# Six seven-product groups for five in the two plain feed-forward stages, with the weights' sums made by accumulating DMAs

## The chip, the cores and the metric

One core of one Trainium2 chip runs the kernel. The metric is the device time in microseconds of one execution, as the median of several. TensorE is written PE in the profile, ScalarE ACT, VectorE DVE, GpSimd POOL, SyncE SP.

## The reference

Two transformer blocks of width 2048 on 256 tokens, one after the other. The first has a state-space and a delta-rule mixer and a feed-forward with a convolution. The second has two plain SwiGLU feed-forwards of hidden width 5632 with a pooling and gated-linear-attention mixer between them. The change concerns the two SwiGLU stages:

```python
def swiglu(h, w_in, w_out):
    gu = h @ w_in
    gate, up = gu[..., :D_FF], gu[..., D_FF:]
    return (jax.nn.silu(gate) * up) @ w_out

def second_block(x, ...):
    h = h + 0.5 * swiglu(rmsnorm_2(h, ffn1_norm[l]), ffn1_w_in[l], ffn1_w_out[l])
    ...
    h = h + 0.5 * swiglu(rmsnorm_2(h, ffn2_norm[l]), ffn2_w_in[l], ffn2_w_out[l])
```

## The kernel before

Every matrix product is made in float32 precision out of three products of a rounded type: an operand is split into a high part (a copy by ScalarE, L126) and a low part (a subtraction by VectorE, L127), and low by low is left out. A weight block is 128 x 1024 float32, 512 KB, loaded by SP (L85, tile wr, four buffers) and split into wh and wl (three buffers each).

A SwiGLU stage is `ffn` (L1050) with `conv_w` None. The hidden width is cut into 11 groups g of 512. `plain(g)` (L1072) makes gate and up of one group with `gemm_tg` (L190): 8 blocks each, and per block 2 k-tiles x 2 halves of the tokens x 3 products = 12 matmuls of 512 columns (L201 to L203, into ptt); it yields after every block. `down_g(c)` (L1091) multiplies one or two groups' hidden tiles (hid) by the down weights in the same manner; its blocks are 8 for chunk 0 and 16 for chunks 1 to 4.

`seven(g)` (L1124) makes the same gate and up with seven products of half size for eight: the weights of a group are a 2 x 2 of halves (gate and up columns, lower and upper half of the k-tiles), and four of the seven products take sums of those quarters against sums of quarters of x, which `x_sums` (L1105) makes once per stage in 8 steps (tiles xf, xs, sx). A group is 28 passes (L1128), each one split into sh and sl (two buffers each) and 6 matmuls of 512 columns (L1133 to L1135, into side), and 30 yields. The weights' sums are made by VectorE (`less`, L1145, into tt, two buffers) from loaded quarters (ws, L1142, three buffers): 16 subtractions a group. Each of the four k-pairs jj makes products 0, 1, 2, 3 in a row, then each makes the three products of the second half.

`together` (L1212) draws one step of the main sequence and one of the sevens in turn. Groups 3, 4, 5, 7 and 9 are sevens, the other six are plain. When a seven or a plain is done, `turn_hidden` (L1056) transposes the result on TensorE (L1062) and splits it into hid tiles; it is put into `pend`, which `gemm_tg` empties in the middle of its next product, or into `after`, which goes to `pend` when `together` ends. The order of each engine's instructions is that of the program, with splits moved ahead by a priority (L124).

Of the kernel before, what the change touches and what calls it, by code (L numbers as in the profile page):

```python
# [18 lines left out]
P = 128  # L19
T = 256  # L20
# [31 lines left out]
def tile_kernel(ctx: ExitStack, tc: tile.TileContext, A, out):  # L52
# [203 lines left out]
    def rstd_of(ps):  # L256

        r = ev.tile([P, T], F32, tag="rstd", bufs=2, name="rstd")
        a = ev.tile([P, T], F32, tag="e0", bufs=3, name="ra")
        b = ev.tile([P, T], F32, tag="e1", bufs=3, name="rb")  # L260
        ts(a, ps[:, :T], EPS, ALU.add)
        act.activation(r, ps[:, :T], AF.Sqrt, bias=epst[:, 0:1])
        newton(r, a, b)
        mul(r, r, b)
        return r
# [480 lines left out]
    def dn_conv(h0):  # L746
        for h in range(h0, h0 + 2):
            for part, t in ((0, qk[h][:, 1, :]), (1, qk[h][:, 0, :]), (2, vv[h])):
                b = 3 * h + part
                c = ev.tile([P, T], F32, tag="e1", bufs=3, name="cc")  # L750
                conv(t, None, lambda i: par("dn_conv", 4 * b + i), 4, c)
                act.activation(t, c, AF.Silu)
                yield
# [296 lines left out]
    def ffn(up, down, hs, rstd, conv_w, scale, fin, gain=None, nxt=None, before_last=None):  # L1050
        with tc.tile_pool(name="hid", bufs=2) as hd:
# [50 lines left out]

            sx = []

            def x_sums():  # L1105
                for j in range(8):
                    f = hd.tile([P, 2, T], F32, tag="g", bufs=1, name="xf")
                    s = hd.tile([P, 4, P], F32, tag="w", bufs=1, name="xs")
                    for i in range(2):
                        add(f[:, i, :], hs[j + 8 * i][:, 0, :].bitcast(F32), hs[j + 8 * i][:, 1, :].bitcast(F32))  # L1110
                    add(s[:, 0, :], f[:, 0, P:], f[:, 1, P:])
                    sub(s[:, 1, :], s[:, 0, :], f[:, 0, :P])
                    sub(s[:, 2, :], f[:, 0, :P], f[:, 0, P:])
                    sub(s[:, 3, :], f[:, 1, :P], s[:, 1, :])
# [9 lines left out]
            def seven(g):  # L1124
# [12 lines left out]
                def block(k2, half, tag=None):  # L1137
                    src = A[up][16 * g + 8 * half + k2]
                    if tag is None:
                        return load_w(src)  # L1140
                    raw = hd.tile([P, 1024], F32, tag=tag, bufs=3, name="ws")
                    sp.dma_start(out=raw, in_=src)  # L1142
                    return raw

                def less(a, b):  # L1145
                    t = hd.tile([P, 1024], F32, tag="tt", bufs=2, name="tt")
                    with tc.high_priority(offset=600):
                        sub(t, a, b)
# [8 lines left out]
                gs, w5, w6 = (hd.tile([P, 512], F32, tag=n, bufs=1, name=n) for n in ("g", "w", "w6"))  # L1157
                for jj in range(4):
                    j, fl = 2 * jj, dict(first=jj == 0, last=jj == 3)
                    b11, b12 = block(jj, 0), block(jj, 1, "ws")  # L1160
                    t1 = less(b12, b11)
                    passes(ps[0], hx(j, 0), b11, **fl)
                    if jj == 3:
                        act.copy(out=w6, in_=ps[0])
                    yield
                    b22 = block(4 + jj, 1, "ws")
                    passes(ps[1], sxs(j, 0), t1, **fl)
                    if jj == 3:
                        add(w5, ps[1], w6)
                    yield  # L1170
                    b21 = block(4 + jj, 0, "ws")
                    t2 = less(b22, t1)
                    passes(ps[2], sxs(j, 1), t2, **fl)
                    if jj == 3:
                        add(gs, ps[2], w6)
                    yield
                    t4 = less(b21, t2)
                    passes(ps[3], hx(8 + j, 1), t4, **fl)
                    if jj == 3:
                        add(w6, ps[3], w6)  # L1180
                    yield
                for jj in range(4):
                    j, fl = 2 * jj, dict(first=False, last=jj == 3)
                    passes(ps[0], hx(8 + j, 0), block(4 + jj, 0, "ws"), **fl)
                    yield
                    b22 = block(4 + jj, 1, "ws")
                    passes(ps[1], sxs(j, 3), b22, **fl)
                    yield
                    passes(ps[2], sxs(j, 2), less(b22, block(jj, 1, "ws")), **fl)
                    yield  # L1190
                rc = late[0]
                t = hd.tile([P, 2, 512], F32, tag="tt", bufs=2, name="gates")
# [3 lines left out]
                add(gs, ps[1], gs)  # L1196
                add(w5, ps[2], w5)
# [6 lines left out]
                if g == 3:  # L1204
# [5 lines left out]
            after = []  # L1210

            def together(seq, sevens):  # L1212

                side_full[0] = True
                a, b = (itertools.chain(*s) for s in (seq, sevens))
                for x, y in itertools.zip_longest(a, b):
                    pass
# [4 lines left out]
            def up_group(c):  # L1222
                tiles = []
                for i in range(max(8 * c - 4, 0), 8 * c + 4):
                    a = ev.tile([P, T], F32, tag="e1", bufs=3, name="fa")
                    b = ev2.tile([P, T], F32, tag="e2", bufs=2, name="fb")
# [22 lines left out]
            if conv_w is None:  # L1249
# [3 lines left out]
                together([first_plain, plain(1), down_g(0), plain(2), down_g(1)], [x_sums(), seven(3), seven(4)])  # L1253
                for c in range(2, 5):
                    together([plain(2 * c + 2), down_g(c)], [seven(2 * c + 1)])
# [428 lines left out]
```

## Time and profile before

| | |
|---|---|
| median of 3 runs | 3290.38 us (3289.5 to 3291.68) |
| profiled execution | 3289.64 us |
| its span | 3287.8 us |
| TensorE busy, granted clock | 99%, 0.999 of full speed |
| first SwiGLU stage | about 1540 to 2265 us of the span |
| second SwiGLU stage | about 2555 to 3287 us |
| sevens mixed in | 1577 to 2200 and 2600 to 3222 us |

A row of the profile gives an instruction's busy time, and for the idle time ahead of it what ended that. Busy times of TensorE overlap from one matmul to the next, so a distance between matmuls is read from their starts.

### The profile page before, as it was taken

The numbers are of one execution on the slowest core, as the hardware profiler recorded it, in microseconds if no ns is written. First come the engines' busy times: TensorE is split into PE (matmuls) and PEld (weight loads), VectorE is DVE, ScalarE is ACT, GpSimd is POOL, SyncE is SP. The second block draws the span as 40 slices with busy tenths as digits, with TensorE's granted clock in tenths as the row PEclk, the third lists the DMA queues.
The fourth block names the chain that finished last, engine by engine and source line by source line (L and its number), as shares of the span: only waits on it lengthen the run. The fifth ranks groups of instructions, "written<-read, shape, count | busy, mean of one in ns | idle before, by whom it ended". The sixth has DMA issues, their size and how long they took to land.

```text
span 3287.8 us, 44587 instructions
## 1 busy us (share of the span) xinstructions
PE 3265.2 (99%) x16530; PEld 2742.9 (83%) x16530; DVE 2588.5 (79%) x3758; ACT 1774.7 (54%) x2523; POOL 4.0 (0%) x22
## 2 busy tenths in 40 slices
PE   9999999999999999999999999999999999999998
PEld 8887988888888888888888888888888888888887
DVE  8999987666877767677987887875786988878876
ACT  4566666445555445455655555545555655555554
POOL 0000000000000000000000000000000000000000
PEclk9999999999999999999999999999999999999999
DMA  6445543365555555556777777765545677777774
GB/s 223 156 152 174 179 144 116 108 225 180 192 187 188 190 188 188 188 187 204 255 247 248 246 247 243 246 197 190 173 146 195 229 243 248 249 245 243 247 253 148
DMA packets 186873, 666.09 MB, mean 203 GB/s; under 512 B 20880, under 2 KB 25488, under 8 KB 186272
## 3 DMA queue, kind: packets, MB, share of 16 engines
q1 hardware_dynamic: 186080, 662.21, 61.3%
q8 instruction: 129, 2.11, 0.3%
q10 hardware_dynamic: 576, 1.05, 0.1%
q14 instruction: 88, 0.72, 0.1%
HBM read 661.08 MB, written 2.10 MB: 202 GB/s over the span
## 4 chain that ended last, share of the span: by engine, by line
PE 94%; DVE 4%; issue 1%; ACT 1%; DMA 0%; SPq 0%; DVEq 0%
PE ptt L201 18%; PE ptt L202 18%; PE ptt L203 18%; PE pt L170 13%; PE pt L172 6%; PE side L1134 4%; PE side L1135 4%; PE side L1133 4%; DVE wl L127 1%; PE pt L135 1%; PE pt L137 1%; PE pt L136 1%; PE pt L245 1%; PE side L874 1%; PE side L885 1%; PE side L620 1%
## 5 line engine op out<-in xcount | busy, mean ns | idle before, releaser
L126 ACT CAST wh<-wr 128x1024 fp32r<-128x1024 f32 x937 | 984.2, 1051 | 1221.9 <-PE ptt L203 839.4
L127 DVE TENSOR_TENSOR wl<-wr,wh 128x1024 fp32r<-128x1024 f32 x937 | 1146.1, 1223 | 539.0 <-ACT wh L126 534.2
L170 PE MATMUL pt<-h,wh 128*128 128x512 f32 x1792 | 632.1, 397 | 0.0
L172 PE MATMUL pt<-h,wl 128*128 128x256 f32 x1792 | 502.5, 281 | 0.0
L201 PE MATMUL ptt<-wh,h 128*128 128x512 f32 x1088 | 428.3, 394 | 0.0
L202 PE MATMUL ptt<-wl,h 128*128 128x512 f32 x1088 | 425.5, 391 | 0.0
L203 PE MATMUL ptt<-wh,h 128*128 128x512 f32 x1088 | 424.2, 390 | 0.0
L202 PE MATMUL ptt<-wl,hid 128*128 128x512 f32 x1040 | 409.0, 394 | 0.0
L201 PE MATMUL ptt<-wh,hid 128*128 128x512 f32 x1040 | 408.4, 393 | 0.5 <-ACT wh L126 0.5
L203 PE MATMUL ptt<-wh,hid 128*128 128x512 f32 x1040 | 408.4, 394 | 0.0
L170 PEld LDWEIGHTS pt<-h,wh 128*128 128x128 f32 x1792 | 336.3, 188 | 80.9 <-issue 1.0
L172 PEld LDWEIGHTS pt<-h,wl 128*128 128x128 f32 x1792 | 338.3, 189 | 0.6
L201 PEld LDWEIGHTS ptt<-wh,h 128*128 128x128 f32 x1088 | 204.2, 188 | 46.7 <-ACT wh L126 1.2
L203 PEld LDWEIGHTS ptt<-wh,h 128*128 128x128 f32 x1088 | 204.3, 188 | 44.0 <-issue 0.4
L202 PEld LDWEIGHTS ptt<-wl,h 128*128 128x128 f32 x1088 | 204.2, 188 | 43.4
L201 PEld LDWEIGHTS ptt<-wh,hid 128*128 128x128 f32 x1040 | 195.4, 188 | 45.7 <-ACT wh L126 1.0
L202 PEld LDWEIGHTS ptt<-wl,hid 128*128 128x128 f32 x1040 | 195.6, 188 | 44.1
L203 PEld LDWEIGHTS ptt<-wh,hid 128*128 128x128 f32 x1040 | 195.4, 188 | 43.6 <-DVE hid L368 0.5
L127 DVE TENSOR_TENSOR sl<-tt,sh 128x1024 fp32r<-128x1024 f32 x160 | 195.9, 1224 | 21.9 <-ACT sh L126 21.3
L126 ACT CAST sh<-tt 128x1024 fp32r<-128x1024 f32 x160 | 168.3, 1052 | 52.9 <-PE side L1135 48.1
L135 PE MATMUL pt<-h,wl 128*128 128x256 f32 x512 | 149.5, 292 | 0.0
L137 PE MATMUL pt<-h,wh 128*128 128x256 f32 x512 | 145.3, 284 | 0.0
(420 smaller groups left out, 4957.9 us busy)
## 6 DMA issues: line engine op xcount, KB each, us to landing
wr<-in_f_up SPq DMA_DIRECT2D x408, 512.0 KB, 4.3
wr<-in_f_down SPq DMA_DIRECT2D x265, 512.0 KB, 4.3
ws<-in_f_up SPq DMA_DIRECT2D x240, 512.0 KB, 4.3
wr<-in_w_qkv SPq DMA_DIRECT2D x48, 512.0 KB, 3.3
wr<-in_w_gs SPq DMA_DIRECT2D x32, 512.0 KB, 3.3
wr<-in_w_gd SPq DMA_DIRECT2D x32, 512.0 KB, 3.3
wr<-in_w_glu SPq DMA_DIRECT2D x32, 512.0 KB, 3.3
wr<-in_w_out SPq DMA_DIRECT2D x32, 512.0 KB, 3.3
```

The lines of the kernel that those rows point to most:

```text
L126: act.copy(out=hi, in_=raw)
L127: dve.tensor_tensor(out=lo, in0=raw, in1=hi.bitcast(F32), op=ALU.subtract)
L135: pe.matmul(ps, wl, xt[:, 0, :], start=first, stop=False)
L137: pe.matmul(ps, wh, xt[:, 0, :], start=False, stop=last)
L170: pe.matmul(ps.rearrange("p a b -> p (a b)"), hi[:, j, :], xts[k].rearrange("p a b -> p (a b)"), start=k == 0, stop=False, skip_group_chec ...
L172: pe.matmul(ps[:, 0, :], lo[:, j, :], xts[k][:, 0, :], start=False, stop=k == n - 1, skip_group_check=True)
L201: pe.matmul(pss[t], xh, hi[:, j, :], start=k == 0, stop=False)
L202: pe.matmul(pss[t], xh, lo[:, j, :], start=False, stop=False)
L203: pe.matmul(pss[t], xl, hi[:, j, :], start=False, stop=k == n - 1)
L1133: pe.matmul(ps, xh, hi[:, i, :], start=first and i == 0, stop=False, skip_group_check=True)
L1134: pe.matmul(ps, xh, lo[:, i, :], start=False, stop=False, skip_group_check=True)
L1135: pe.matmul(ps, xl, hi[:, i, :], start=False, stop=last and i == 1, skip_group_check=True)
```

## The change

Group 8 becomes a seven too, so a stage has six sevens (3, 4, 5, 7, 8, 9) and five plain groups. In a seven, `less` and the ws tiles go. A base quarter is loaded by SP into a tt tile (five buffers), and between two products GpSimd's queue adds the next quarter to the tile with an accumulating DMA, so the tile goes through base, base + one, + two, + three quarters. Since a DMA only adds, some sums have the other sign, which `x_sums` and the end of `seven` take up. The k-pairs go two by two, (0, 1) and (2, 3), with their products in turn, so that one pair's product lies between two of the other's. `together` draws the sevens from one sequence over the whole stage: 4/3 steps for each main step, 0.6 while x's sums are made. Buffers move: e1 of the pool ev goes to the stage's pool, and its other users take e0; xf, xs, gs and w5 have two buffers.

```diff
--- before.py
+++ after.py
@@ -257,7 +257,7 @@
 
         r = ev.tile([P, T], F32, tag="rstd", bufs=2, name="rstd")
         a = ev.tile([P, T], F32, tag="e0", bufs=3, name="ra")
-        b = ev.tile([P, T], F32, tag="e1", bufs=3, name="rb")
+        b = ev.tile([P, T], F32, tag="e0", bufs=3, name="rb")
         ts(a, ps[:, :T], EPS, ALU.add)
         act.activation(r, ps[:, :T], AF.Sqrt, bias=epst[:, 0:1])
         newton(r, a, b)
@@ -747,7 +747,7 @@
         for h in range(h0, h0 + 2):
             for part, t in ((0, qk[h][:, 1, :]), (1, qk[h][:, 0, :]), (2, vv[h])):
                 b = 3 * h + part
-                c = ev.tile([P, T], F32, tag="e1", bufs=3, name="cc")
+                c = ev.tile([P, T], F32, tag="e0", bufs=3, name="cc")
                 conv(t, None, lambda i: par("dn_conv", 4 * b + i), 4, c)
                 act.activation(t, c, AF.Silu)
                 yield
@@ -1100,18 +1100,19 @@
 
 
 
+
             sx = []
 
             def x_sums():
                 for j in range(8):
-                    f = hd.tile([P, 2, T], F32, tag="g", bufs=1, name="xf")
-                    s = hd.tile([P, 4, P], F32, tag="w", bufs=1, name="xs")
+                    f = hd.tile([P, 2, T], F32, tag="g", bufs=2, name="xf")
+                    s = hd.tile([P, 4, P], F32, tag="w", bufs=2, name="xs")
                     for i in range(2):
                         add(f[:, i, :], hs[j + 8 * i][:, 0, :].bitcast(F32), hs[j + 8 * i][:, 1, :].bitcast(F32))
-                    add(s[:, 0, :], f[:, 0, P:], f[:, 1, P:])
-                    sub(s[:, 1, :], s[:, 0, :], f[:, 0, :P])
+                    sub(s[:, 0, :], f[:, 1, P:], f[:, 0, P:])
+                    stt(s[:, 1, :], s[:, 0, :], -1.0, f[:, 0, :P], ALU.mult, ALU.subtract)
                     sub(s[:, 2, :], f[:, 0, :P], f[:, 0, P:])
-                    sub(s[:, 3, :], f[:, 1, :P], s[:, 1, :])
+                    stt(s[:, 3, :], f[:, 1, :P], -1.0, s[:, 1, :], ALU.mult, ALU.subtract)
                     e = []
                     for i in range(2):
                         t = hp.tile([P, 2, 2, P], F32R, tag=f"h{j + 8 * i}", name=f"sx{j}_{i}")
@@ -1134,18 +1135,12 @@
                         pe.matmul(ps, xh, lo[:, i, :], start=False, stop=False, skip_group_check=True)
                         pe.matmul(ps, xl, hi[:, i, :], start=False, stop=last and i == 1, skip_group_check=True)
 
-                def block(k2, half, tag=None):
-                    src = A[up][16 * g + 8 * half + k2]
-                    if tag is None:
-                        return load_w(src)
-                    raw = hd.tile([P, 1024], F32, tag=tag, bufs=3, name="ws")
-                    sp.dma_start(out=raw, in_=src)
-                    return raw
-
-                def less(a, b):
-                    t = hd.tile([P, 1024], F32, tag="tt", bufs=2, name="tt")
-                    with tc.high_priority(offset=600):
-                        sub(t, a, b)
+                def src(k2, half):
+                    return A[up][16 * g + 8 * half + k2]
+
+                def base(k2, half):
+                    t = hd.tile([P, 1024], F32, tag="tt", bufs=5, name="tt")
+                    sp.dma_start(out=t, in_=src(k2, half))
                     return t
 
                 def hx(k, t):
@@ -1154,67 +1149,61 @@
                 def sxs(j, c):
                     return lambda i: sx[j + i][c]
 
-                gs, w5, w6 = (hd.tile([P, 512], F32, tag=n, bufs=1, name=n) for n in ("g", "w", "w6"))
-                for jj in range(4):
-                    j, fl = 2 * jj, dict(first=jj == 0, last=jj == 3)
-                    b11, b12 = block(jj, 0), block(jj, 1, "ws")
-                    t1 = less(b12, b11)
-                    passes(ps[0], hx(j, 0), b11, **fl)
-                    if jj == 3:
-                        act.copy(out=w6, in_=ps[0])
-                    yield
-                    b22 = block(4 + jj, 1, "ws")
-                    passes(ps[1], sxs(j, 0), t1, **fl)
-                    if jj == 3:
-                        add(w5, ps[1], w6)
-                    yield
-                    b21 = block(4 + jj, 0, "ws")
-                    t2 = less(b22, t1)
-                    passes(ps[2], sxs(j, 1), t2, **fl)
-                    if jj == 3:
-                        add(gs, ps[2], w6)
-                    yield
-                    t4 = less(b21, t2)
-                    passes(ps[3], hx(8 + j, 1), t4, **fl)
-                    if jj == 3:
-                        add(w6, ps[3], w6)
-                    yield
-                for jj in range(4):
-                    j, fl = 2 * jj, dict(first=False, last=jj == 3)
-                    passes(ps[0], hx(8 + j, 0), block(4 + jj, 0, "ws"), **fl)
-                    yield
-                    b22 = block(4 + jj, 1, "ws")
-                    passes(ps[1], sxs(j, 3), b22, **fl)
-                    yield
-                    passes(ps[2], sxs(j, 2), less(b22, block(jj, 1, "ws")), **fl)
-                    yield
+                gs, w5, w6 = (hd.tile([P, 512], F32, tag=n, bufs=b, name=n) for n, b in (("g", 2), ("w", 2), ("w6", 1)))
+                for pair in ((0, 1), (2, 3)):
+                    tt = {jj: base(jj, 0) for jj in pair}
+                    for n in range(4):
+                        for jj in pair:
+                            xa = (hx(2 * jj, 0), sxs(2 * jj, 0), sxs(2 * jj, 1), hx(8 + 2 * jj, 1))[n]
+                            passes(ps[n], xa, tt[jj], first=jj == 0, last=jj == 3)
+                            if n < 3:
+                                pool_e.dma_start(out=tt[jj], in_=(src(jj, 1), src(4 + jj, 1), src(4 + jj, 0))[n],
+                                                 accum_op=ALU.add)
+                            if jj == 3 and n == 0:
+                                act.copy(out=w6, in_=ps[0])
+                            elif jj == 3:
+                                add((w5, gs, w6)[n - 1], ps[n], w6)
+                            yield
+                for pair in ((0, 1), (2, 3)):
+                    tt = {jj: base(4 + jj, 1) for jj in pair}
+                    for n in (1, 2, 0):
+                        for jj in pair:
+                            xa = (hx(8 + 2 * jj, 0), sxs(2 * jj, 3), sxs(2 * jj, 2))[n]
+                            passes(ps[n], xa, tt[jj] if n else load_w(src(4 + jj, 0)), first=False, last=jj == 3)
+                            if n == 1:
+                                pool_e.dma_start(out=tt[jj], in_=src(jj, 1), accum_op=ALU.add)
+                            yield
                 rc = late[0]
-                t = hd.tile([P, 2, 512], F32, tag="tt", bufs=2, name="gates")
+                t = hd.tile([P, 2, 512], F32, tag="tt", bufs=5, name="gates")
                 act.activation(t[:, 0], ps[0], AF.Silu, scale=rc[:, 0:1])
                 add(t[:, 1], ps[2], w6)
                 act.activation(t[:, 1], t[:, 1], AF.Silu, scale=rc[:, 1:2])
-                add(gs, ps[1], gs)
-                add(w5, ps[2], w5)
+                stt(gs, gs, -1.0, ps[1], ALU.mult, ALU.subtract)
+                stt(w5, w5, -1.0, ps[2], ALU.mult, ALU.subtract)
                 a = gs, w5
                 for i in range(2):
                     stt(a[i], a[i], rc[:, i : i + 1], t[:, i], ALU.mult, ALU.mult)
                 yield
                 new_ys(g)
                 return_turn = lambda: turn_hidden(a, ys[g])
-                if g == 3:
+                if g in (3, 7, 8):
                     pend.append(return_turn)
                 else:
                     after.append(return_turn)
                 yield
 
             after = []
-
-            def together(seq, sevens):
+            others = itertools.chain(x_sums(), *(seven(g) for g in (3, 4, 5, 7, 8, 9)))
+            due = [0.0]
+
+            def together(*seq):
 
                 side_full[0] = True
-                a, b = (itertools.chain(*s) for s in (seq, sevens))
-                for x, y in itertools.zip_longest(a, b):
-                    pass
+                for _ in itertools.chain(*seq):
+                    due[0] += 4 / 3 if len(sx) == 8 else 0.6
+                    while due[0] >= 1.0:
+                        due[0] -= 1.0
+                        next(others, None)
                 side_full[0] = False
                 pend.extend(after)
                 after.clear()
@@ -1222,8 +1211,8 @@
             def up_group(c):
                 tiles = []
                 for i in range(max(8 * c - 4, 0), 8 * c + 4):
-                    a = ev.tile([P, T], F32, tag="e1", bufs=3, name="fa")
-                    b = ev2.tile([P, T], F32, tag="e2", bufs=2, name="fb")
+                    a = hd.tile([P, T], F32, tag="e1", bufs=3, name="fa")
+                    b = hd.tile([P, T], F32, tag="e2", bufs=2, name="fb")
                     pss = [gemm2(wsrc(up, 2 * i + j), hs) for j in range(2)]
                     if i == 0:
                         late[0] = late[0]()
@@ -1250,9 +1239,15 @@
                 first_plain = plain(0)
                 for _ in range(4):
                     next(first_plain)
-                together([first_plain, plain(1), down_g(0), plain(2), down_g(1)], [x_sums(), seven(3), seven(4)])
-                for c in range(2, 5):
-                    together([plain(2 * c + 2), down_g(c)], [seven(2 * c + 1)])
+                together(first_plain, plain(1), down_g(0), plain(2), down_g(1))
+                together(down_g(2))
+                together(plain(6), down_g(3))
+                due[0] = 2.0
+                together(plain(10), down_g(4))
+                for _ in others:
+                    pass
+                pend.extend(after)
+                after.clear()
                 if before_last:
                     before_last()
                 for _ in down_g(5):
```

## Rows read from the trace of the kernel before

**Rows 1.** The page's busy times: us (share of the span) and instructions, with granted clock.

```profile
PE 3265.2 (99%) x16530; PEld 2742.9 (83%) x16530; DVE 2588.5 (79%) x3758; ACT 1774.7 (54%) x2523; POOL 4.0 (0%) x22
...
PEclk9999999999999999999999999999999999999999
```

**Rows 2.** Windows: us; busy PE, PEld, DVE, ACT, POOL; clock; DMA share; GB/s.

```profile
1577.00:2200.00 623.00, 623.00 (x2742) 507.54 (x2742) 518.08 (x519) 333.12 (x345) 0.00 (x0) 1.00 0.75 243
2600.00:3222.00 622.00, 622.00 (x2737) 506.76 (x2736) 511.74 (x491) 329.55 (x338) 0.00 (x0) 1.00 0.75 245
1540.00:2265.00 725.00, 724.73 (x3207) 591.41 (x3207) 596.25 (x652) 392.50 (x440) 1.55 (x7) 1.00 0.73 239
```

**Rows 3.** Timeline of TensorE, 1730.9 to 1739.6: start, busy us, line.

```profile
1731.07 0.39 PE L1133 MATMUL side<-sh,h 128*128 128x512 f32 x1
...
1732.47 0.39 PE L201 MATMUL ptt<-wh,h 128*128 128x512 f32 x1
...
1735.21 0.39 PE L1133 MATMUL side<-sh,h 128*128 128x512 f32 x1
...
1739.35 0.39 PE L1133 MATMUL side<-sh,sx 128*128 128x512 f32 x1
```

**Rows 4.** Timeline of TensorE: a hid block beside side passes.

```profile
1795.88 0.40 PE L201 MATMUL ptt<-wh,hid 128*128 128x512 f32 x1
...
1798.67 0.39 PE L1133 MATMUL side<-sh,sx 128*128 128x512 f32 x1
```

**Rows 5.** Groups of instructions in 1577 to 2200: count, busy us, mean ns, idle.

```profile
L203 PE MATMUL ptt<-wh,h 128*128 128x512 f32 x334 | 130.1, 390 | 0.0
...
L201 PE MATMUL ptt<-wh,hid 128*128 128x512 f32 x274 | 108.1, 395 | 0.0
...
L1133 PE MATMUL side<-sh,sx 128*128 128x512 f32 x160 | 63.5, 397 | 0.0
...
L1133 PE MATMUL side<-sh,h 128*128 128x512 f32 x120 | 47.7, 397 | 0.0
```

**Rows 6.** Timelines of ScalarE and VectorE: one split of a side pass.

```profile
1732.67 1.05 ACT L126 CAST sh<-tt 128x1024 fp32r<-128x1024 f32 x1 [0.35 <-PE side L1135]
...
1733.75 1.23 DVE L127 TENSOR_TENSOR sl<-tt,sh 128x1024 fp32r<-128x1024 f32 x1 [0.17 <-ACT sh L126]
```

**Rows 7.** Groups by form, whole span: half of the weights' subtractions.

```profile
L368 DVE TENSOR_TENSOR tt<-ws,tt 128x1024 f32<-128x1024 f32 x80 | 98.0, 1225 | 2.0
```

**Rows 8.** Waits in 1577 to 2200: us in all, times, longest.

```profile
ACT wh L126 <- PE ptt L203: 232.8, 140, 3.1
```

**Rows 9.** DMA issues: count, KB each, median us to landing; then ws: min/median/max.

```profile
ws<-in_f_up SPq DMA_DIRECT2D x240, 512.0 KB, 4.3
...
cmat<-in_s_c SPq DMA_DIRECT2D x1, 1024.0 KB, 7.8
gb<-in_gain SPq DMA_DIRECT2D x1, 1024.0 KB, 5.5
wpl<-in_w_pool SPq DMA_DIRECT2D x1, 1024.0 KB, 6.7
...
DMA to landing us min/median/max: 3.0/4.3/7.5
```

**Rows 10.** Timeline 2214.5 to 2218: the last chunk's transposes and the next matmul.

```profile
2216.00 0.27 PE L1062 MATMUL side<-ident,w 128*128 128x128 f32 x1
...
2216.54 0.98 PE L201 MATMUL ptt<-wh,hid 128*128 128x512 f32 x3 [0.27 <-ACT wh L126]
```

**Rows 11.** By tile (cc, lowh): count, ns min/median/max, first and last start.

```profile
L675 ACT ACTIVATE cc<-qk,prm x16: 492/504/512, 70.1 to 229.0; 128x256 f32<-128x256 f32 x16
...
L752 ACT ACTIVATE v<-cc x8: 400/410/420, 98.7 to 238.4; 128x256 f32<-128x256 f32 x8
...
L231 ACT ACTIVATE lowh<-pt x112: 363/375/398, 809.3 to 2474.3; 128x256 f32<-128x256 f32 x112
```

## The prediction

> **What bounds the kernel now.** I read the busy shares and the clock first, then the stretches of the two plain feed-forward stages, then the start times of single matmuls, then who waits for whom. The reader sees TensorE busy for 99% of the span at the full granted clock [rows 1], and in the two stretches where the sevens are mixed in it is busy for all of 623.00 and 622.00 us [rows 2]. VectorE has 518 of 623 us there and ScalarE 333 [rows 2]. So time falls here only with fewer matmul columns, or rises where TensorE is made to wait.
>
> The busy time of one matmul (390 to 397 ns) is no price, because matmuls overlap. I price them by start times. A side pass of six matmuls runs from 1731.07 to 1732.47, 1.40 us; a block of twelve on h from 1732.47 to 1735.21, 2.74 us [rows 3]; one on hid from 1795.88 to 1798.67, 2.79 us [rows 4]. Check: the first stretch holds 83.4 h blocks, 68.5 hid blocks and 140 passes [rows 5], 228.5 + 191 + 196 = 616 us, and some 80 transposes of 0.11 us make it 624 of 623.
>
> **Part 1, the group that becomes a seven.** In each of the two stages group 8 changes from plain (16 blocks, 43.8 us) to seven (28 passes, 39.2 us): 4.6 us less on the path, 9.2 us for both. Its 12 extra splits per stage (ScalarE 1.05, VectorE 1.23 us each [rows 6]) lie beside matmuls.
>
> **Part 2, the subtractions.** 16 a group, 160 in all at 1.225 us [rows 7], 196 us of VectorE, go. VectorE was not late for TensorE in these stretches, so this is worth nothing by itself; it pays for part 1's splits. I count nothing.
>
> **Part 3, the accumulating loads, which decide.** 192 of them (16 a group, 12 groups) go to the Pool queue, which is idle here [rows 1, 2]: only the next accumulating load stands behind a waiting one. Each waits for both halves of the split before it (ScalarE's copy, VectorE's subtraction) and the next split of that tile waits for its landing. SP's queue gets 8 base loads a group, each held only until one of five tt buffers is free. A late split stands in order on ScalarE ahead of copies for the main chain. Those start when the buffer frees, 1.66 us after the engine's last work on average (232.8 us in 140 waits [rows 8]), three blocks ahead, some 13.9 - 2.8 = 11 us, so the side passes are hit first.
>
> How much time has such a load? The copy of a side split starts 0.20 us after the pass that frees its buffer (1732.47 to 1732.67), the subtraction ends at 1733.75 + 1.23 = 1734.98, 2.31 us after the copy's start, and the pass that uses it begins at 1739.35, two steps on [rows 3, 6]. At 4/3 sides per main step two side steps last 1.5 x 2.76 + 2 x 1.40 = 6.94 us in the mean. So a split is ready 6.94 - 1.40 - 0.20 - 2.31 = 3.03 us ahead of its pass, and from its end to the next copy of the same tile there are 6.94 - 2.31 = 4.63 us. If a load takes L from request to landing, each link is late by L - 4.63; the first half of a pair has three links, so TensorE waits 3 (L - 4.63) - 3.03 per pair. It is nothing up to **L = 5.64 us**; beyond, with 2 pairs x 6 groups x 2 stages = 24, each further us costs 72 us. The uneven steps (5.56 and 8.32 us between a tile's passes) give the same point, since what a chain loses in its links it has in its first lead. The second half of a pair has one link and waits only from L = 7.66.
>
> The trace has no accumulating load. The nearest rows: a load of the same 512 KB in these stages lands after 4.3 us; a load that reads 1024 KB, the bytes this one reads in all, after 5.5, 6.7 and 7.8 us in the three places where there is one [rows 9]. So L lies between 4.3 and 7.8; I take **5.5**, the shortest of the three, since only half of the bytes come from HBM (the other half lies in the tt tile). With it TensorE doesn't wait, by a margin of 0.14 us. At 4.3 likewise; at 6.7 the waits are 24 x 3.18 = 76 us, at 7.8 24 x (6.48 + 0.14) = 159 us. Descriptors written by Pool instead of SP may add to L; nothing in the rows prices it, and the upper end stands for it.
>
> What the row shows of the engines: DMA is busy 0.73 of 725 us in the first stage [rows 2] for 324 loads, 1.63 us of all 16 engines each. The Trainium skill (Collectives: The Full Stack, The bandwidth ceiling: the fold count and why AG ≠ RS ≠ AR) says that a summing transfer emits two read descriptors per piece on one ring, and so moves at half the rate. No run here shows it. It speaks against this change, and is priced as rival 1.
>
> **Part 4, the rate.** Main steps are 68, 16, 32 and 32; side steps 8 + 6 x 30 = 188. Fourteen main steps at 0.6 draw the eight sums, then 72, 21, 43 and 44 are drawn: 188, none left over. The sums' two fused operations (some 0.35 for 0.29 us) lie on VectorE beside matmuls. One thing is new on the path: the down product of chunk 2 now follows with no up group between, so group 4's transposes stand immediately ahead of their use. The like place in the last chunk shows the cost: 0.54 us from 2216.00 to 2216.54 where 0.11 would do [rows 10], 0.43 us, twice: 0.9 us. It can't be under nothing, since transposes only stand closer to their use; above, I allow twice the 0.43 us.
>
> **Part 5, buffers.** e0 takes e1's uses in ev. The convolutions (70.1 to 238 us) and the halves of pt (809 us on) [rows 11] never meet, and the statistics of the start take two of three buffers, so nothing waits. The first feed-forward keeps three and two buffers. But moved tiles change addresses, and the start-to-start time of equal matmuls differs by tile, 2.74 or 2.79 us per block, and 1.40 for six where 1.37 is half a block [rows 3, 4]. If all 336 passes ran at 1.37 it would be 10 us less, if all 160 up blocks ran at 2.79, 8 us more. I take no change and keep -10 and +8 for the range.
>
> **Sum.** The profiled execution took 3289.64 us (span 3287.8), 0.74 under the median of three. 3289.64 - 9.2 + 0.9 = 3281.3, and with 0.74, **3282 us**.
>
> **The rivals.**
> *Rival 1, the second read is a full second transfer.* L = 4.3 + 1.6 = 5.9 us, 24 x (3 x 1.27 - 3.03) = 19 us of waits: 3301 us, slower by 0.3%; nearby values run from 3288 to 3325. For it: the load must read its destination, and the share would go from 0.73 to 0.73 x 432/324 = 0.97. Against it: 0.97 is still under one, and a 4.3 us landing is mostly not engine time. By the rule of the Trainium skill's Collectives page above, this is the one that comes out; the trace can't say.
> *Rival 2, the landing passes 6.3 us.* Pool writes descriptors, and the accumulating packets queue among SP's. From L = 6.3 on the time is over 3329 us; at 6.7 it is 3358, at 7.8, 3441. This one ends clearly slower, and decides from the same 5.64. For it: the rows of 1024 KB at 6.7 and 7.8, and the longest 512 KB landing of 7.5 [rows 9]. Against: 1024 KB all from HBM is more than this load reads there.
> *Rival 3, the products are saved and don't show.* The loads fit, but addresses, transposes, and now and then a late split give 5 to 10 us back: 3289 us, no change that can be told.
>
> **How the numbers follow.** Forecast 0.45 (its own range 3273 to 3290), rival 1 0.15, rival 2 0.18, rival 3 0.22. A measurement of this kernel can tell some 0.2%, 6.6 us: faster means under 3283.8, slower over 3297.0. Faster: 0.38 of the forecast's and 0.04 of rival 3's, 0.42. Slower: 0.09 of rival 1, all of rival 2, 0.04 of rival 3, 0.31. Same: 0.27. The range goes from 3273 (addresses at their best) to 3350, which leaves out 0.02 below and some two thirds of rival 2 above, 0.14 in all.
>
> **What the profile would show.** Right: some 48 matmuls of 512 columns fewer, TensorE without gaps in both stretches, no subtraction on tt, landings of the accumulating loads at or under 5.6 us. Rival 1 or 2: a side copy on ScalarE that waits for the tt load, for longer from the second to the fourth product of a pair, and TensorE idle ahead of the fourth, in 24 places. Rival 3: no such waits, but starts 5 ns further apart. I am wrong in the step itself if landings are late and TensorE doesn't wait, since then the splits run further ahead than two buffers let them.

## The result and the profile after

The changed kernel takes 3493.36 us (median of four runs, 3491.77 to 3499.15) against 3291.03 us before: a ratio of 1.0617 [1.0604, 1.0630], 202 us slower. The forecast of 3282 us and its range up to 3350 us were wrong. The profiled execution took 3499.15 us, of which the span is 3497.4.

The first view is the page of the changed kernel: busy us (share) and instructions of each engine, and two DMA queues (packets, MB, share of 16 engines' time). The last line is the view of the cores, with the mean granted clock.

```profile
PE 3340.2 (96%) x16482; PEld 2753.3 (79%) x16482; DVE 2422.5 (69%) x3634; ACT 1781.4 (51%) x2549; POOL 169.9 (5%) x214
...
q1 hardware_dynamic: 161888, 574.12, 48.6%
q0 software_dynamic: 27648, 100.68, 16.9%
...
core 0: 3497.4 us, clock 0.985
```

TensorE has the 48 matmuls fewer that were foretold [rows 1], and VectorE 166 us less work. Yet TensorE is *busy* 75 us longer, and idle for the rest. The queue of the accumulating loads (q0) holds 192 loads: 16.9% of 3497.4 us is 591 us, 3.08 us of all 16 DMA engines for each.

Where does it stand still? The windows view of the changed kernel gives most of the first of the two stretches (columns as in [rows 2]):

```profile
1600.00:2280.00 680.00, 612.89 (x2520) 474.69 (x2519) 399.27 (x390) 309.60 (x325) 78.53 (x91) 0.97 0.83 216
```

Before, TensorE was busy for all of such a stretch [rows 2]; now 67 of 680 us are idle, and the clock is 0.97. The view of waits of the changed kernel (us in all, times, longest) says for what:

```profile
ACT sh L126 <- DMA tt<-in_f_up: 494.4, 181, 8.3
...
PE side L1134 <- ACT sh L126: 82.4, 55, 6.0
...
PE side L1135 <- DVE sl L127: 50.1, 76, 0.8
```

The reader sees the chain that the prediction named: a landing is late, ScalarE's copy of the side tile (sh) waits for it 181 times, and TensorE waits for the two halves of the split, 82.4 + 50.1 = 132.5 us in 131 waits. For the main chain of these stages the same view has 0.5 us in 2 waits; the side passes are hit, as foretold.

The DMA view of the changed kernel (count, KB, median us from issue to landing) has the term that decided:

```profile
tt<-in_f_up POOLq DMA_DIRECT2D x192, 512.0 KB, 7.1
tt<-in_f_up SPq DMA_DIRECT2D x96, 512.0 KB, 6.1
wr<-in_f_up SPq DMA_DIRECT2D x384, 512.0 KB, 3.5
```

One link can be read off the timelines of ScalarE, VectorE and Pool (start, busy us; in brackets idle time before and its releaser):

```profile
1999.35 1.05 ACT L126 CAST sh<-tt 128x1024 fp32r<-128x1024 f32 x1 [2.04 <-DMA tt<-in_f_up]
...
2000.43 1.23 DVE L127 TENSOR_TENSOR sl<-tt,sh 128x1024 fp32r<-128x1024 f32 x1 [2.36 <-ACT sh L126]
...
2001.95 0.86 POOL L1160 DMA_DIRECT2D tt<-in_f_up  x1 [3.86 <-DVE sl L127]
...
2007.77 1.05 ACT L126 CAST sh<-tt 128x1024 fp32r<-128x1024 f32 x1 [2.81 <-DMA tt<-in_f_up]
```

The split ends at 2000.43 + 1.23 = 2001.66, Pool issues 0.29 us later, and the next copy of the same tile starts at 2007.77. That is 6.11 us where the prediction had found room for 4.63, so this link is late by 1.48 us, and its two side steps last 2007.77 - 1999.35 = 8.42 us in place of 6.94.

### The profile page after: what moved, and what is told of

Read it like the earlier page. It is cut to its first block, busy times and chain, and to the rows that moved or that the text cites. A ratio compares the mean times of both kernels' runs of the same rounds, so it can differ in the third digit from the quotient of the medians.

```text
span 3497.4 us, 44585 instructions
## 1 busy us (share of the span) xinstructions
PE 3340.2 (96%) x16482; PEld 2753.3 (79%) x16482; DVE 2422.5 (69%) x3634; ACT 1781.4 (51%) x2549; POOL 169.9 (5%) x214
## 3 DMA queue, kind: packets, MB, share of 16 engines
q0 software_dynamic: 27648, 100.68, 16.9%
## 4 chain that ended last, share of the span: by engine, by line
PE 58%; DMA 17%; issue 12%; DVE 8%; ACT 3%; POOL 1%; SPq 0%; POOLq 0%; ACTq 0%; DVEq 0%
DMA tt<-in_f_up 16%; PE pt L170 12%; PE ptt L201 10%; PE ptt L203 10%; PE ptt L202 10%; PE pt L172 6%; DVE sl L127 2%; DVE wl L127 2%; ACT sh L126 2%; PE pt L135 1%; PE pt L137 1%; PE pt L136 1%; PE side L1135 1%; PE side L1136 1%; ACT wh L126 1%
## 5 line engine op out<-in xcount | busy, mean ns | idle before, releaser
L127 DVE TENSOR_TENSOR wl<-wr,wh 128x1024 fp32r<-128x1024 f32 x905 | 1104.7, 1221 | 521.7 <-ACT wh L126 519.2
L126 ACT CAST wh<-wr 128x1024 fp32r<-128x1024 f32 x905 | 949.6, 1049 | 941.1 <-PE ptt L203 547.6
L127 DVE TENSOR_TENSOR sl<-tt,sh 128x1024 fp32r<-128x1024 f32 x288 | 351.3, 1223 | 454.3 <-ACT sh L126 452.8
L126 ACT CAST sh<-tt 128x1024 fp32r<-128x1024 f32 x288 | 300.8, 1049 | 566.8 <-DMA tt<-in_f_up 494.4
L172 PE MATMUL pt<-h,wl 128*128 128x256 f32 x1792 | 502.8, 281 | 0.0
L201 PE MATMUL ptt<-wh,h 128*128 128x512 f32 x960 | 383.9, 400 | 0.0
L202 PE MATMUL ptt<-wl,h 128*128 128x512 f32 x960 | 379.2, 395 | 0.0
L203 PE MATMUL ptt<-wh,h 128*128 128x512 f32 x960 | 378.4, 394 | 0.0
L1160 POOL DMA_DIRECT2D tt<-in_f_up x144 | 124.4, 864 | 2647.8 <-DVE sl L127 2479.1
L201 PEld LDWEIGHTS ptt<-wh,h 128*128 128x128 f32 x960 | 183.9, 192 | 41.8 <-ACT wh L126 1.2
L203 PEld LDWEIGHTS ptt<-wh,h 128*128 128x128 f32 x960 | 183.0, 191 | 40.5 <-issue 0.4
L1134 PE MATMUL side<-sh,sx 128*128 128x512 f32 x384 | 160.3, 418 | 52.4 <-ACT sh L126 52.0
```

What stands on the lines that cost most here:

```text
L126: act.copy(out=hi, in_=raw)
L127: dve.tensor_tensor(out=lo, in0=raw, in1=hi.bitcast(F32), op=ALU.subtract)
L172: pe.matmul(ps[:, 0, :], lo[:, j, :], xts[k][:, 0, :], start=False, stop=k == n - 1, skip_group_check=True)
L201: pe.matmul(pss[t], xh, hi[:, j, :], start=k == 0, stop=False)
L202: pe.matmul(pss[t], xh, lo[:, j, :], start=False, stop=False)
L203: pe.matmul(pss[t], xl, hi[:, j, :], start=False, stop=k == n - 1)
```

## The experiments

The theory (A): each load lands later than its link has room, three links of one tile in a row add up, and TensorE waits at the end of the chain. The rivals: (B) DMA throughput, since the loads simply load the DMA engines too much; (C) Pool's way of issuing them, and not the addition. Beside these three it could be the products or the rate themselves, with no part of the loads in it. Each ratio is to the kernel before, timed together with that run.

**One: the same loads without the addition.** This takes the addition from A, and leaves C as it is; the kernel leaves out the sums of the weights.

```diff
-  pool_e.dma_start(out=tt[jj], in_=(src(jj, 1), ...)[n], accum_op=ALU.add)
+  pool_e.dma_start(out=tt[jj], in_=(src(jj, 1), ...)[n])
```

(and the same in the second half of a group)

> The 192 loads of the changed kernel stay on the Pool queue with the same waits, but replace the tile's contents and add nothing (the weights' sums are left out). Theory A, the addition makes the landing late (7.1 us, packets of double length) and three late links in a row stall TensorE: the landing falls to 5.0 to 5.6 us and the time to 3280 to 3300 us. Theory B, the DMA engines are full: the share of the Pool queue halves, the time falls to the same values, and the landing of SP's loads falls too. Theory C, Pool's own issue and descriptors make the landing late, not the addition: landing still at 6.5 us or more, time over 3400 us.

Measured: 3319.13 us, 1.0087 [1.0072, 1.0102]. From its page and its DMA and wait views:

```profile
q0 software_dynamic: 27648, 100.68, 8.8%
...
tt<-in_f_up POOLq DMA_DIRECT2D x192, 512.0 KB, 4.5
...
PE side L1135 <- DVE sl L127: 11.5, 19, 0.8
PE side L1134 <- ACT sh L126: 9.6, 9, 2.9
```

Without the addition the landing falls from 7.1 to 4.5 us, the waits from 132.5 to 21 us, and 174 of the 202 us are gone. A load from Pool's queue by itself lands nearly as one from SP did (4.5 for 4.3 us [rows 9]), so C is not the main thing. But with a median under the threshold of 5.64 us there are still waits, which the next run prices.

**Two: no chain.** Each product has a fresh tile, loaded by SP; the sums of the weights are left out.

```diff
-  pool_e.dma_start(out=tt[jj], in_=(src(jj, 1), src(4 + jj, 1), src(4 + jj, 0))[n], accum_op=ALU.add)
+  tt[jj] = base(*((jj, 1), (4 + jj, 1), (4 + jj, 0))[n])
...
-  pool_e.dma_start(out=tt[jj], in_=src(jj, 1), accum_op=ALU.add)
+  tt[jj] = base(jj, 1)
```

> Each product's quarter is loaded by SP into a fresh tt tile of the five, so no load waits for a split of the same tile and nothing is added (the weights' sums are left out); six groups and the order of the change stay. It measures the price of the saved products by itself. If the terms of the sum besides the landing were right: 3279 to 3286 us, TensorE without gaps. If the sixth group gains nothing by itself: 3289 us or more.

Measured: 3284.22 us, 0.9977 [0.9967, 0.9986]. The windows view of this run:

```profile
1600.00:2180.00 580.00, 580.00 (x2547) 470.47 (x2546) 409.31 (x393) 322.84 (x330) 0.00 (x0) 1.00 0.76 258
```

TensorE is busy for all of the stretch. So it isn't the products or the rate: products, rate, transposes and buffers together give -7.8 us, where the prediction's other terms gave -9.2 + 0.9 = -8.3. All that the change lost lies in the loads into a used tile. And the first experiment, 35 us above this one, shows that such loads cost something though the median fits: of its landings one in ten took over 6.35 us, read from the single loads of its trace.

**Three: the same additions, spaced.** Four tiles take turns in place of two, so that each has the time of four side steps between two of its products. The accumulating loads stay, all 192.

```diff
-  for pair in ((0, 1), (2, 3)):
+  for pair in ((0, 1, 2, 3),):
```

(in both halves of a group)

> The changed kernel with its four k-pairs in one quad in place of two pairs, so that three other passes instead of one lie between two products of one tile; as many accumulating loads, as many bytes, five tiles as before. Theory A (late links of one chain): a link then has 13.9 - 2.3 = 11.6 us for a landing of 7.5 us, TensorE hardly waits, 3280 to 3295 us. Theory B (DMA engines full): the traffic is the same, 3400 us or more.

Measured: 3286.48 us, 0.9983 [0.9973, 0.9992]. The DMA view, and the windows view of the same stretch as in the second experiment:

```profile
tt<-in_f_up POOLq DMA_DIRECT2D x192, 512.0 KB, 10.5
...
1600.00:2180.00 580.00, 579.58 (x2542) 469.48 (x2541) 407.82 (x393) 319.83 (x330) 80.84 (x94) 1.00 0.91 256
```

This separates A from B. The DMA engines are fuller than in any stretch so far (0.91), a landing takes 10.5 us, half as long again as in the changed kernel, and TensorE idles 0.42 of 580 us. By the prediction's method a side step lasts 6.94 / 2 = 3.47 us, a link now has 4 x 3.47 - 2.31 = 11.57 us of room, and 10.5 + 0.39 (0.29 from the split's end to Pool's issue, 0.10 from the landing to the copy) fits. A late landing costs nothing by itself; late for its link it does. This version computes all that the changed kernel computes and beats both kernels, the one before by 0.17%.

**Four: six groups, with the weights' sums on VectorE** as in the kernel before.

```diff
-  passes(ps[n], xa, tt[jj], first=jj == 0, last=jj == 3)
-  if n < 3:
-      pool_e.dma_start(out=tt[jj], in_=..., accum_op=ALU.add)
...
+  t1 = less(b12, b11)
+  ...
+  passes(ps[1], sxs(j, 0), t1, **fl)
```

> Six groups at the rates of the change, but the sums made by VectorE's subtractions as before the change, in its order and with its buffers (ws three, tt two). Tests whether the accumulating loads were needed for the sixth group. If VectorE can carry it (about 0.9 busy while sevens are mixed in): 3279 to 3290 us. If VectorE becomes the bound: TensorE waits for sl and wl, over 3300 us.

Measured: 3286.25 us, 0.9982 [0.9973, 0.9991]. The windows view:

```profile
1577.00:2190.00 613.00, 612.60 (x2690) 497.22 (x2689) 540.65 (x529) 340.66 (x349) 0.00 (x0) 1.00 0.77 259
```

VectorE has 540.65 of 613 us and TensorE doesn't wait for it. So the sixth group didn't need the accumulating loads at this rate: with them spaced or without them, the time is the same within its spread.

**Five: five groups at one side step for each main step**, with the accumulating loads. Here a link has more room, 8.32 - 2.31 = 6.01 us, and the lead is 4.41.

```diff
-  due[0] += 4 / 3 if len(sx) == 8 else 0.6
+  due[0] += 1.0
...
-  *(seven(g) for g in (3, 4, 5, 7, 8, 9))
+  *(seven(g) for g in (3, 4, 5, 7, 9))
```

> The accumulating loads in pairs as in the change, but five groups (8 plain again) and one side step for each main step. Theory A: two side steps last 2 x 2.76 + 2 x 1.40 = 8.32 us, a link 6.0 us, the lead 4.4 us, so three links bear landings of 7.5 us in the mean (3 x 1.5 - 4.4 = 0.2 us of wait per pair), and only the longer landings stall: 3293 to 3325 us. Theory B' (an accumulating load costs TensorE or the DMA engines something by itself, whatever the spacing): 160 of 192 loads leave five sixths of the 200 us, 3440 us or more.

Measured: 3367.78 us, 1.0229 [1.0213, 1.0245], well over what was expected. The DMA and wait views:

```profile
tt<-in_f_up POOLq DMA_DIRECT2D x160, 512.0 KB, 7.3
...
PE side L1135 <- DVE sl L127: 26.5, 41, 0.8
PE side L1134 <- ACT sh L126: 15.8, 20, 1.6
```

The landing is nearly the changed kernel's, and the formula with the full lead gives 3 x (7.3 + 0.39 - 6.01) - 4.41 = 0.6 us for a pair, 13 us for 20 pairs. The waits are 42.3 us, and the time 76 us over before. The single loads and splits of this trace, taken in the program's order, show two reasons (medians). The landing goes by the place in the chain: the loads behind a tile's first product take 8.6 to 10.8 us, those behind the second and third 5.7 to 8.2. And the first split of a group is ready only 1.8 us ahead of its pass, not 4.41. With the leads and landings put in tile by tile, the formula gives 1.5 to 3.6 us, where the waits are 42.3 / 20 = 2.1 us for a pair.

**Six and seven: one half of a group each.** The sixth experiment keeps the accumulating loads of the second halves (one link each), the seventh those of the first halves (three links); the other half has fresh tiles, and leaves out its sums, as in the second experiment. The first edit below is six, the second seven.

```diff
-  pool_e.dma_start(out=tt[jj], in_=(src(jj, 1), src(4 + jj, 1), src(4 + jj, 0))[n], accum_op=ALU.add)
+  tt[jj] = base(*((jj, 1), (4 + jj, 1), (4 + jj, 0))[n])
-  pool_e.dma_start(out=tt[jj], in_=src(jj, 1), accum_op=ALU.add)
+  tt[jj] = base(jj, 1)
```

> The changed kernel with its accumulating loads kept only in the second half of a group (4 of 16, one link in a row); in the first half each product's quarter is loaded by SP into a fresh tile (those sums are left out). Theory A: one link of 7.5 us fits into 4.63 + 3.03 = 7.66 us, 3284 to 3300 us. If each link stalls by itself: 48 of 192 loads, 3284 + 0.25 x 209 = 3336 us.

> The complement: accumulating loads only in the first half (12 of 16, three links in a row); the second half's are loaded by SP into fresh tiles (those sums are left out). Theory A: nearly all of the 209 us over the kernel without a chain stay, 3430 to 3495 us. If each link stalls by itself: 3284 + 0.75 x 209 = 3441 us, which this run can't tell apart, but the one before does.

Measured: 3307.99 us, 1.0046 [1.0030, 1.0063], for the second halves alone, a little over what was expected; 3457.31 us, 1.0502 [1.0486, 1.0518], for the first halves alone, as expected. Waits of the sixth, then of the seventh:

```profile
PE side L1135 <- DVE sl L127: 7.6, 13, 1.8
PE side L1134 <- ACT sh L126: 6.3, 6, 1.8
```

```profile
PE side L1134 <- ACT sh L126: 67.1, 48, 4.8
PE side L1135 <- DVE sl L127: 42.4, 62, 0.8
```

Over the kernel without a chain they cost 23.8 and 173.1 us, 197 of the 209 us of both together. Three links in a row are seven times as dear as one, where links that stall each by itself would make it three times: the lateness adds up, as A says. The single link was foretold to wait only from 7.66 us, and waits a little at a median of 6.9; again landings above the median.

**Eight and nine: a third buffer for the splits.** If the lead is what lacks, a third sh and sl buffer lets a split start one step sooner. The room for it comes from one tt buffer, and from g and w; nine makes the same cuts without the third buffer.

```diff
-  to = [hd.tile([P, 1024], F32R, tag=n, bufs=2, name=n) for n in ("sh", "sl")]
+  to = [hd.tile([P, 1024], F32R, tag=n, bufs=3, name=n) for n in ("sh", "sl")]
...
-  t = hd.tile([P, 1024], F32, tag="tt", bufs=5, name="tt")
+  t = hd.tile([P, 1024], F32, tag="tt", bufs=4, name="tt")
```

> The changed kernel with three buffers each for sh and sl in place of two (room from one tt tile and the second xf, xs, gs and w5). Splits may run one step further ahead, 3.47 us more lead at the start of a chain, the link stays 4.63 us. Theory A: per pair 3 x (7.5 - 4.63) - 6.5 = 2.1 us of wait in place of 5.6, 24 pairs: 3284 + 51 us and some loss of clock, 3325 to 3400 us. If the lead doesn't matter (each landing counts): 3480 us or more.

> The control of the run with three split buffers: the changed kernel with four tt tiles and one buffer for xf, xs, gs and w5, but two for sh and sl. If the smaller room made that run slower, this one is at 3524 us or more, and the third split buffer did nothing or helped. If it is at 3493 us as the changed kernel, the third split buffer itself cost some 30 us. A third split buffer can help only if the splits behind a late one may pass it; ScalarE's copies stand in one order, so I expect no help: 3515 to 3535 us here.

Measured: 3524.68 us, 1.0708 [1.0692, 1.0724], with three; 3494.84 us, 1.0614 [1.0595, 1.0634], with the cuts alone. Both expectations failed: the cuts cost nothing, and the third buffer costs 30 us. Waits of the ninth, then of the eighth with the third buffer:

```profile
PE side L1134 <- ACT sh L126: 77.6, 51, 6.3
PE side L1135 <- DVE sl L127: 48.0, 73, 0.9
```

```profile
PE side L1134 <- ACT sh L126: 67.3, 49, 4.8
PE side L1135 <- DVE sl L127: 52.1, 75, 2.0
...
PE ptt L201 <- ACT hid L1064: 19.5, 6, 6.2
```

The waits of the side passes fall only from 125.6 to 119.4 us, and a new one appears: the main chain's matmul waits for hid, a copy of ScalarE's for that chain. The longest of the six, on ScalarE:

```profile
1813.01 1.04 ACT L126 CAST sh<-tt 128x1024 fp32r<-128x1024 f32 x1 [8.36 <-DMA tt<-in_f_up]
...
1814.91 1.06 ACT L1064 CAST hid<-side 128x512 fp32r<-128x512 f32 x2
```

A side copy whose tile has not landed stands at the head of ScalarE's queue, and what stands behind it, copies of the main chain among them, is late instead. So it is in four of the six waits, 14.9 of 19.5 us; in the other two a seven's last activation (gates), waiting for VectorE, stands there. Between the two profiled executions lie 23.4 us (3519.4 and 3496.0 us of span), and TensorE's idle time makes 19.6 of them.

**Ten: seven groups of seven, spaced as in three**, at 16/9 side steps for each main step, 2 in the last stretch. This asks how far the spacing goes.

```diff
-  for pair in ((0, 1), (2, 3)):
+  for pair in ((0, 1, 2, 3),):
...
-  *(seven(g) for g in (3, 4, 5, 7, 8, 9))
+  *(seven(g) for g in (3, 4, 5, 6, 7, 8, 9))
...
-  due[0] += 4 / 3 if len(sx) == 8 else 0.6
+  due[0] += rate[0] if len(sx) == 8 else 0.6
```

> The quads with a seventh seven (group 6), at 16/9 side steps per main step and 2 in the last stretch. Saves 9.2 us more of matmuls; a link has 4 x 1.40 + 2.25 x 2.76 - 2.31 = 9.5 us for a landing of 10.5 us or more, and the loads fill 236 x 1.55 + 112 x 3.0 = 702 us of the DMA engines in a stage of some 707 us. If the quads' room holds also here: 3276 to 3282 us. If the landings pass the room or the engines are full: TensorE waits, 3290 to 3380 us.

Measured: 3354.78 us, 1.0191 [1.0174, 1.0208]. Its DMA view and windows:

```profile
tt<-in_f_up POOLq DMA_DIRECT2D x224, 512.0 KB, 9.7
...
1600.00:2200.00 600.00, 574.03 (x2451) 452.89 (x2450) 412.60 (x401) 322.64 (x335) 92.33 (x107) 0.99 0.92 252
```

A side step now lasts 2.76 x 9/16 + 1.40 = 2.95 us, so a link has 4 x 2.95 - 2.31 = 9.5 us, and a landing takes 9.7. The DMA share is that of the third experiment (0.92 for 0.91), the landing a little shorter, and here TensorE waits. The three links of a tile's first half, each from a split's end to the next copy (medians), add up to 36.6 us in three, for 3 x 11.57 = 34.7 us of room and 3.03 of lead, and to 32.2 us here, for 28.5 and 1.99: the first fits and the second doesn't. So the room tells the two runs apart where the DMA share and the landing don't; what else a seventh group does was not varied by itself.

## Why the prediction was wrong

**The step that failed is the length L of an accumulating load.** Part 3 took 5.5 us, the shortest of three 1024 KB loads [rows 9], because half of the bytes don't come from HBM. Measured: 7.1 us in the median, and from the split's end to the next copy of the tile, with 0.29 us to Pool's issue and 0.10 from the landing, 7.48. The two others of those three rows, 6.7 and 7.8, were the near ones. They were single loads in places with other work, and no row stood behind the reason that favoured the shortest; it was also the only one of the three that kept the forecast on its side of the threshold, by 0.14 us.

**The formula around L came out in size, not in place.** 24 x (3 x (7.48 - 4.63) - 3.03) = 24 x 5.52 = 132 us of waits; the rows sum to 132.5. That agreement is luck. The formula lets TensorE idle ahead of the fourth product of a pair alone, and in second halves only from 7.66 us on. Taken one by one in the program's order, the waits ahead of the first to the fourth product are 4, 39, 26 and 43 us, and the second halves have 20. The start of one group shows why (SP, ScalarE, VectorE, TensorE, Pool, ScalarE, TensorE):

```profile
1941.88 0.87 SPq L1143 DMA_DIRECT2D tt<-in_f_up  x1
...
1948.33 1.05 ACT L126 CAST sh<-tt 128x1024 fp32r<-128x1024 f32 x1
...
1949.42 1.23 DVE L127 TENSOR_TENSOR sl<-tt,sh 128x1024 fp32r<-128x1024 f32 x1
...
1950.70 0.50 PE L1135 MATMUL side<-sl,h 128*128 128x512 f32 x1
...
1950.94 0.86 POOL L1160 DMA_DIRECT2D tt<-in_f_up  x1 [23.61 <-DVE sl L127]
...
1960.51 1.04 ACT L126 CAST sh<-tt 128x1024 fp32r<-128x1024 f32 x1 [5.22 <-DMA tt<-in_f_up]
...
1961.61 0.50 PE L1134 MATMUL side<-sh,sx 128*128 128x512 f32 x1 [3.24 <-ACT sh L126]
```

**The lead of 3.03 us isn't there** for the first tile of a group. Its base load is asked for by SP only some 8 us ahead of the pass, and its split is done at 1949.42 + 1.23 = 1950.65, 0.05 us before the matmul that reads it (0.06 in the median of the 12 groups). The second experiment has the same 0.05 us and no waits, so this costs nothing by itself; but a chain that starts so waits from its first late link on, here 3.24 us ahead of the second product. **And L is no single number.** In a group's first pair the loads behind the first product take 8.3 and 10.6 us (first and second tile, medians), those behind the second 5.9 and 5.7, behind the third 7.0; why the first take longest isn't shown. The first tile of a group's first pair has 64 of the 132 us. That lateness adds up along a tile, that the side passes are hit, and that more room takes the loss away is what the runs show; the threshold of 5.64 us for every pair is not.

**So the median was the wrong measure of L near the threshold.** The first experiment's median of 4.5 us lies over 1 us under 5.64, and yet it loses 35 us. Of its 21 us of waits 17 stand at that same first tile, which has no lead and whose first link takes a landing of 6.0 us; the other 4 us are spread over the other tiles, where landings go up to 8.7 us.

**Two terms were missing.** The time over the kernel without a chain is 209 us, of which the waits are 132. The mean clock is 0.985 where that kernel's trace has 0.998: 3497 x 0.013, some 45 us. And a matmul after a wait doesn't overlap the one ahead of it: it is busy 0.39 us where matmuls in a row start about 0.23 us apart [rows 3], so each of 131 waits costs more than its row tells, by the single starts 0.20 us, 27 us in all. Delays too short for a row of idle time cost the same way: at the full clock it happens 198 times that the start behind a matmul of 512 columns comes over 0.27 us after it with no row of idle time, against 75 times without the chain, which is 16 us. 132 + 45 + 27 + 16 = 220, where the two traces lie 215 us apart (3497.4 and 3282.7), so nothing of size is left over. The first and the sixth experiment bear the last two out at the clock of 0.998: TensorE is busy 11.7 and 9.2 us longer than without the chain, for 28 and 19 waits. None of these terms was varied by itself.

**Of the rivals**, the second came, "the landing passes 6.3 us", with a chance of 0.18; its price for 7.8 us, 3441, lacked the two terms, and the range, which left two thirds of this rival out, ended far too low. Of its reasons, that Pool writes descriptors is not the main one: without the addition Pool's loads land after 4.5 us. That the packets queue was not tested by itself. The first rival, a full second transfer, was right in its cause. The engines' time for a load went from 8.8% of 3315.9 us / 192 = 1.52 us to 3.08, a factor of 2.0. The Trainium skill (Collectives: The Full Stack, The bandwidth ceiling: the fold count and why AG ≠ RS ≠ AR) says that the summing transfer of a ReduceScatter reads both operands over one ring and so moves at half the rate; these two shares agree with it. Where the rival failed is its price: it added the engine time of one more transfer (1.6 us) to a landing of 4.3, while the landing grew by 7.1 - 4.5 = 2.6 us. Pool's own issuing instruction makes 0.33 of them (0.86 us with the addition, 0.53 without); the rest may be loads of both queues standing behind each other, which no run shows.

**What held:** parts 1, 2, 4 and 5 in their sum (the second experiment, -7.8 us for -8.3), and of the signs named for rivals 1 and 2 the copies of the side tile that wait for the landing. The other sign, TensorE idle ahead of the fourth product in 24 places, did not: it waits in 131 places, ahead of the second product nearly as long. That the side passes are hit first was foretold as well.

## What to carry to other kernels

When a load is put into a chain that reuses one tile, work out the room of a link (steps between two uses, less the work on the tile) and compare it with the landings at each place of the chain, the late ones above all, not with one median; look up as well what lead the chain starts with. Where no trace has such a load, a forecast that rests on a margin of 0.14 us rests on nothing. The cure is room, not speed: more tiles in turn between two loads of the same tile took the whole loss back with longer landings and fuller DMA queues, while a further buffer behind an engine that works in order only moved the wait into the main chain. Before moving sums from VectorE, see whether it is late for anyone; at a share of 0.88 it was not.

## What the runs showed of the hardware

The granted clock fell in the midst of work. In the changed kernel about two dozen stretches of 3.4 to 6.8 us have about half of it, the level of 1.2 GHz, though TensorE is busy in most of them. The windows view of one, and the timeline of TensorE around it:

```profile
2031.40:2034.80 3.40, 3.40 (x10) 2.63 (x9) 3.27 (x4) 2.83 (x3) 0.00 (x0) 0.51 0.47 143
```

```profile
2029.80 0.49 PE L1134 MATMUL side<-sh,sx 128*128 128x512 f32 x1 [0.97 <-ACT sh L126]
...
2031.06 0.50 PE L1135 MATMUL side<-sl,sx 128*128 128x512 f32 x1 [0.77 <-DVE sl L127]
...
2032.20 0.63 PE L1135 MATMUL side<-sl,sx 128*128 128x512 f32 x1
2032.63 0.63 PE L1136 MATMUL side<-sh,sx 128*128 128x512 f32 x1
2033.06 0.63 PE L201 MATMUL ptt<-wh,h 128*128 128x512 f32 x1
...
2036.19 0.39 PE L202 MATMUL ptt<-wl,h 128*128 128x512 f32 x1
2036.41 0.39 PE L203 MATMUL ptt<-wh,h 128*128 128x512 f32 x1
```

Two waits, of 0.97 and 0.77 us, lie close together; after them matmuls start 0.43 us apart and not 0.22, with no wait between. By 2036 the old spacing is back. So the waits cost more than their own time. In the runs with next to no such waits (two, three and four) the mean clock is 0.998 or 0.999, with 61 and 72 waits (five and ten) 0.996, and with 110 to 131 (seven, nine, eight and the changed kernel) 0.988, 0.982, 0.981 and 0.985. It isn't a fixed price for a wait.

The landing of one kind of load is no constant of it: 7.1 us with two tiles in turn, 10.5 with four, at a DMA share of 0.83 and 0.91. The same 192 accumulating loads take 16.9% of 3497.4 us in the one and 16.2% of 3284.7 in the other, 3.08 and 2.77 us each: the engines don't work longer on them, so it seems that they stand longer in the queues, with more of them asked for early. That is argued, not shown.
